# Where a small product stands in a long in-projection: decode rows in the middle of each unit, and 64 products ahead of the first tokens

## The chip, the cores and the metric

The kernel runs on one core of a Trainium2 chip. The time is device time in microseconds (us) of one launch, taken as the median of several runs; before the change it is 1346.13 us over 3 runs, which lie between 1345.68 and 1351.22. Engines are named as the profile names them: PE is the matmul engine (PEld its weight loads), DVE the vector engine, ACT the scalar engine, POOL the general engine and SP the one that issues most of the DMAs. A trailing q (SPq, ACTq) is an engine's instruction queue.

## What is computed

One step of a hybrid decoder layer, on a prompt of 2048 tokens and on eight decode rows (one new token each, with 512 cached positions in four pages). Both pass the same norm, the same input projection and the same output projection:

```python
def branch_inputs(x, g_norm, w_in, b_f, g_q, g_k, g_v):
    h = rms_norm(x, g_norm)
    p = h @ w_in
    q, k, v, fz, za, u, gv, zc = jnp.split(p, SPLIT_IDX, axis=-1)
...
def merge(x, attn, za, mix, u, zc, w_out):
    a = attn.astype(x.dtype).reshape(B, S, D_ATT) * jax.nn.silu(za)
    m = (u * mix.astype(x.dtype)).reshape(B, S, D_CHK) * jax.nn.silu(zc)
    return x + jnp.concatenate([a, m], axis=-1) @ w_out
```

`q`, `k` and `v` go into causal attention with a forgetting term (8 heads of 64), `gv` is normalised and mixed inside chunks of 128 positions by a lower triangular matrix for each of four groups. The model width is 1024, and `p` has 3592 columns. The outputs are the two results and the keys, values, log forget values and normalised `gv` rows.

## The kernel before

It has three phases: the in-projection (0 to about 590 us), the attention (to about 1160 us) and the output projection. The change is in the first.

**The in-projection.** The 3592 columns of `w_in` are cut into eight *units* (`SEGS`), which run in the order 3, 0, 1, 2, 4, 5, 6, 7; their widths are 392, 384, 384, 384 and then 512 each. Every float32 operand is split into a high and a low part, so that one product is three matmuls for each of the eight tiles `k` of 128 rows of the model width: high by high, low by high and high by low (`wh`, `wl` for weights, `hh`, `hl` for tokens). A product of 24 matmuls fills one PSUM bank with the tag `acc`; there are four such banks, and they are used in turn. So the product that comes fourth after another one takes the same bank, and it cannot start before the earlier one has been read out.

In units 3, 0, 1, 2 (`qkv_tile`) and 4 (`gv_tile`) a product is one tile of 128 tokens by the unit's columns. They go one tile after another, and only tiles 14 and 15 go side by side. In units 5, 6 and 7 the columns go to PSUM's partitions and 512 tokens lie along a bank: two `cp` halves by two `f` halves make four groups, each of two products side by side. In units 5 and 6 these are `u` (read out by DVE in L507) and `zc` (ACT, then DVE in L490), in unit 7 two of `za` (both ACT, then L490). `together` interleaves the products of a group step by step, one `k` of each in turn. In unit 4 and its follow-up the mixing products of `gv` (tag `pm`, eight matmuls of 256 columns) come between.

**The decode rows.** `sample_products` multiplies the eight decode rows, whose high and low parts lie side by side in `hTs`, by a unit's columns: 16 matmuls into one `acc` bank. ACT copies the half of the high rows (L377), DVE adds the other half (L378), and POOL stores the sum (L381). Before the change it is the first member of a unit's last group: with tiles 14 and 15, or with `cp` 1, `f` 1.

**Weights of the next unit.** `load_unit` is given in the middle of a unit. SP loads pieces of 128 rows into three buffers `raw` (L291); ACT or POOL makes the high part with the norm's gain (L253, L255), DVE the low part (L256). A unit's `wh` and `wl` take eight buffers of eleven, so some of the next unit's parts wait until PE has done the last group's product with the present ones.

**What sets the order.** PE's instructions stand in the order in which the program gives them. The program keeps a clock of the work given to PE (`Pe.clock`), and `later` puts other work at a due time on that clock. The order on the other engines comes from a scheduler that simulates a timeline while the program is built. Each engine then works its queue strictly in that order. From unit 4 on the scores of the decode rows against their cached keys run beside the in-projection: SP loads a page of keys `kb`, POOL multiplies (L660), DVE sums (L661).

Of the kernel before, what the change touches and what calls it, by code (L numbers as in the profile page):

```python
# [19 lines left out]
P = 128  # L20
# [3 lines left out]
NT = SEQ // P  # L24
# [11 lines left out]
NCP = 2  # L36
# [7 lines left out]
STLAG = 5000.0  # L44
STLAST = 2500.0
SLAG = 3000.0
LAG = 6400.0
AVB = 8
WK = 11
# [29 lines left out]
def hymba_step(ctx, tc, x_prompt, x_sample, cache_k, cache_v, cache_logf, page_table, g_norm, w_in,  # L79
# [32 lines left out]
    def tname(t):  # L112
        cnt[0] += 1
        return f"{t}_{cnt[0]}"

    def s8(dt=F32, t="s8"):
        return big.tile([P, 2048], dt, tag="s8", name=tname(t))

    def s4(dt=F32, t="s4"):
        return med.tile([P, D], dt, tag="s4", name=tname(t))  # L120
# [4 lines left out]
    def s2(dt=F32, t="s2"):  # L125
        return wk.tile([P, 512], dt, tag="t2", name=tname(t))
# [6 lines left out]
    def bank(tag, n=512):  # L133
        pool, bufs = pool_of[tag]
        return pool.tile([P, n], F32, tag=tag, bufs=bufs, name=tname(tag))
# [10 lines left out]
    def pe(ns):  # L146
        Pe.clock += ns

    def later(ns, fn):
        Pe.given += 1  # L150
        Pe.waiting.append((Pe.clock + ns, Pe.given, fn))
        Pe.waiting.sort(key=lambda w_: w_[:2])
# [20 lines left out]
    def mm(out, lhsT, rhs, start, stop, ns):  # L173
        Pe.last = nc.tensor.matmul(out, lhsT, rhs, start=start, stop=stop).ins  # L174
        pe(ns)

    def transpose(out, in_, idn):
        Pe.last = nc.tensor.transpose(out, in_, idn).ins  # L178
        pe(109)
# [9 lines left out]
    identb = const.tile([P, P], BF16, name="identb")  # L189
# [50 lines left out]
    def split(hi, lo, src, eng):  # L240

        if eng == "act":
            nc.scalar.copy(hi, src)  # L243
        elif eng == "dve":
            nc.vector.tensor_copy(hi, src)
        else:
            nc.gpsimd.tensor_scalar(hi, src, 1.0, 0.0, op0=ALU.mult, op1=ALU.add)
        nc.vector.tensor_tensor(lo, src, hi.bitcast(F32), op=ALU.subtract)  # L248
# [53 lines left out]
    def norm_tile(xa, xv, rows=P):  # L302
        nc.sync.dma_start(xv, xa)
        junk = wk.tile([P, D], BF16, tag="t2", name=tname("junk"))[:rows]
        ss = small(1)[:rows]
        nc.scalar.activation(junk, xv, AF.Square, bias=zero1[:rows], accum_out=ss)
        r = rstd_of(ss, 1, rows, 1.0 / D)
        nc.vector.tensor_scalar(xv, xv, r, None, op0=ALU.mult)
        return xv
# [3 lines left out]
    def norm_prompt(i):  # L313
        if i < NT - 4:
            if i % 2 == 0:
                xpair[i // 2] = s8(t="xp")
            xv = xpair[i // 2][:, (i % 2) * D:(i % 2 + 1) * D]
        else:
            xv = s4(t="xt")
        return norm_tile(x[i * P:(i + 1) * P], xv)  # L320
# [82 lines left out]
    def qkv_tile(u, unit, i):  # L403
# [7 lines left out]
        if m:  # L411
# [4 lines left out]
            def scale():  # L416
# [8 lines left out]
                def turn():  # L425
# [5 lines left out]
                    for src, dst in ((hi, qk_hi), (lo, qk_lo)):  # L431
                        nc.sync.dma_start(dst[f0:f0 + cols, t0:t0 + P].rearrange("(j p) t -> p j t", p=P),
                                          src.rearrange("p (j t) -> p j t", t=P).bitcast(F32))
                later(LAG + LAG2[i] - RLAG, turn)
            later(RLAG, scale)
# [11 lines left out]
    def gv_tile(unit, i):  # L447
# [24 lines left out]
        later(RLAG, scale)  # L472
        later(LAG + LAG2[i], mix)

# [451 lines left out]
    def shifts(h, c, part):  # L926
# [9 lines left out]
        def turn():  # L936
# [9 lines left out]
            later(3500, store)  # L946
        later(SLAG, turn)

# [218 lines left out]
    with ExitStack() as p1:  # L1167
        psa = p1.enter_context(tc.tile_pool(name="psa", bufs=2, space=PSUM, reuse_waits="tile"))
        pool_of.update(acc=(psa, 4), tp=(psa, 2), pm=(psa, 2))

        normd = {0: norm_prompt(0)}
        raws = [s8(t="wraw") for _ in range(2)]
        units = {order[0]: load_unit(SEGS[order[0]], [raws[k // 4][:, (k % 4) * 512:(k % 4 + 1) * 512]
                                                      for k in range(KT)],
                                     lambda: turn_tile(0, normd.pop(0)))}
        normd[1] = norm_prompt(1)
        nc.sync.dma_start(pt_sb, page_table.rearrange("b n -> (b n)").unsqueeze(0))
        nc.sync.dma_start(gqk[:, 0], g_q[0].partition_broadcast(P))
        nc.sync.dma_start(gqk[:, 1], g_k[0].partition_broadcast(P))
        nc.vector.tensor_scalar(gqk[:, 0], gqk[:, 0], -SCALE, None, op0=ALU.mult)  # L1180
        nc.sync.dma_start(bfb, b_f[0].partition_broadcast(P))
        nc.sync.dma_start(gvT, g_v[0].rearrange("(g c) -> c g", g=NG), allow_slow_non_contiguous=True)
        nc.sync.dma_start(bsb.rearrange("p g t -> p (g t)"),
                            b_s[0].rearrange("g t -> (g t)").partition_broadcast(P))
        nc.sync.dma_start(w00, w_s[0][:, 0, 0].partition_broadcast(DB), allow_slow_non_contiguous=True)

        wsr = s2(t="wsr")
        wsr3 = wsr.rearrange("t (g s) -> t g s", g=NG)
        nc.gpsimd.dma_start(wsr3, w_s[0].rearrange("g t s -> t g s"))
        nc.gpsimd.affine_select(wsr3, wsr3, pattern=[[0, NG], [-1, P]], compare_op=ALU.is_ge, fill=0.0,  # L1190
                                base=0, channel_multiplier=1)

        def mix_weights():
            wsp = bank("tp")
            for g in range(NG):
                transpose(wsp[:, g * P:(g + 1) * P], wsr[:, g * P:(g + 1) * P], ident)
            wsp3 = wsp.rearrange("s (g t) -> s g t", g=NG)
            split(wst[:, :, :P], wst[:, :, P:], wsp3, "act")

        for pos, u in enumerate(order):  # L1200
            unit = units.pop(u)
            nxt = order[pos + 1] if pos + 1 < len(order) else None
            group = []
            if u <= 4:
                for i in range(NT):
                    if pos == 0:
                        if i + 2 < NT:
                            normd[i + 2] = norm_prompt(i + 2)
                        if i + 1 == NT - 1:
                            pump(all_=True)  # L1210
                            turn_tile(i + 1, normd.pop(i + 1))
                        elif i + 1 < NT - 1:
                            later(TLAG if i else TLAG0, lambda i=i: turn_tile(i + 1, normd.pop(i + 1)))
                        if i == 2:
                            mix_weights()
                            sample = norm_tile(xs, s4(t="xt")[:DB], DB)
                            later(20000, lambda: turn_sample(sample))
                    group.append(qkv_tile(u, unit, i) if u <= 3 else gv_tile(unit, i))
                    if i == NT - 2:
                        group.insert(0, sample_products(unit, WID[u], SEGS[u]))  # L1220
                    if u == 4 and i == KSTART:
                        Pe.decode, Pe.steps = Pe.clock, chain(decode_qk(), decode_scores())
                    if i not in (PAIRS if pos else (NT - 2,)):
                        together(*group)
                        group = []
                    if i == (NT - 2 if pos == 0 else 7):
                        units[nxt] = load_unit(SEGS[nxt])
                if u == 3:
                    gates()
            else:  # L1230
                for cp in range(NCP):
                    for f in range(2):
                        if u < 7:
                            mx = s2(t="mxu")
                            of = 2 * (u - 5) + f
                            group = [u_steps(unit, f * P, of, cp, "acc", mx),
                                     zc_steps(unit, 256 + f * P, of, cp, "acc", mx)]
                        else:
                            group = [za_steps(unit, g * P, g, cp, "acc") for g in (2 * f, 2 * f + 1)]
                        if cp == NCP - 1 and f == 1:  # L1240
                            group.insert(0, sample_products(unit, WID[u], SEGS[u]))
                        together(*group)
                    if u == 7 and cp == 0:
                        heads[0] = load_keys(0)
                        load_values(heads[0])
                        fw = s8(F32R, "fw")
                        first.append(fill_weights(OZA, (fw[:, :D], fw[:, D:])))
                        Pe.side = Pe.clock + SSTART
                    if cp == 0 and nxt is not None:
                        units[nxt] = load_unit(SEGS[nxt])  # L1250
        for _ in Pe.steps:
            pass
        pump(all_=True)
# [79 lines left out]
```

## Time and profile before

| | |
|---|---|
| median of 3 runs | 1346.13 us |
| lowest and highest run | 1345.68, 1351.22 us |
| the profiled execution | 1347.51 us, its span 1345.8 us |
| mean granted clock of PE | 0.987 |
| PE, PEld, DVE, ACT, POOL busy | 97%, 75%, 53%, 32%, 43% of the span |
| chain of work that ended last | PE 85%, DMA 6%, DVE 4% |
| idle time of PE by releaser | 10.0 us for the first tokens, 4.9 us in three waits for L378, the rest in waits of at most 2.5 us |

The profile is of one execution. A row of its timeline gives the start, the duration, engine, line, operation, output and inputs, and in brackets the idle time of the engine just ahead with what ended it. Matmuls run into one another, so the cost of one in a row of them is the distance between two starts, and not its duration. A row of the waits gives who waited for whom, the sum in us, how many times, and the longest. A row of the windows gives, for a stretch of time, busy us (and instructions) of PE, PEld, DVE, ACT and POOL, then the clock that PE was granted, the share of the DMA engines and GB/s.

### The profile page before, as it was taken

To read this page: it belongs to the slowest core of one execution; us is meant where nothing else is said; L and a number is where in the kernel's file an instruction comes from. 1 tells how busy PE (TensorE), PEld (TensorE's weight loads), DVE (VectorE), ACT (ScalarE), POOL (GpSimd) and SP (SyncE) were. 2 spreads that over 40 slices of the span, in tenths; PEclk is the share of its full clock that TensorE was granted. 3 is DMA by queue.
4 is the path that set the end of the run, shared out by engine and by line. 5 is a ranking of instruction groups with operands and counts; after the bars stand their busy time and mean duration, and the time that the engine had idled before them with its cause. 6 is when DMAs were issued, how large, how long until landed. Compare 5 with 4: busy or idle time off the path is not lost.

```text
span 1345.8 us, 19516 instructions
## 1 busy us (share of the span) xinstructions
PE 1304.6 (97%) x6544; PEld 1006.6 (75%) x6544; DVE 706.9 (53%) x1328; ACT 433.1 (32%) x781; POOL 574.6 (43%) x679
## 2 busy tenths in 40 slices
PE   6999999999999999999999999999999998999998
PEld 5999999999887877866666566666656664688877
DVE  4346654534678544266586555566565774322321
ACT  5542332222222111114453344434444456310100
POOL 3113343423223554416776666676757466400000
PEclk9999999999999999999998899999999998999999
DMA  6644353555113665634254854666375645463221
GB/s 217 188 119 112 87 142 116 155 140 158 52 48 99 187 184 148 159 97 127 78 138 85 181 138 126 177 182 169 95 192 135 172 119 196 135 238 117 107 77 49
DMA packets 170805, 183.09 MB, mean 136 GB/s; under 512 B 39402, under 2 KB 125866, under 8 KB 169138
## 3 DMA queue, kind: packets, MB, share of 16 engines
q1 hardware_dynamic: 166818, 173.08, 46.7%
q10 hardware_dynamic: 3488, 8.39, 1.6%
q8 instruction: 52, 0.85, 0.3%
q14 instruction: 47, 0.39, 0.1%
q0 software_dynamic: 400, 0.38, 0.1%
HBM read 121.53 MB, written 60.28 MB: 135 GB/s over the span
## 4 chain that ended last, share of the span: by engine, by line
PE 85%; DMA 6%; DVE 4%; ACT 2%; issue 1%; SPq 1%; POOL 1%; ACTq 0%; DVEq 0%; POOLq 0%
PE acc L174 36%; PE sc L174 15%; PE av L174 14%; PE fl L174 10%; PE tp L174 5%; PE tp L178 3%; PE pm L174 1%; DVE mn L918 1%; ACT p L982 1%; DMA xp<-in_x_prompt_dram 1%; DMA raw<-in_w_in_dram 1%; DMA q<-qk_hi 1%; DMA k<-qk_lo 1%; DMA q<-qk_lo 1%; DMA mrow<-mt 0%
## 5 line engine op out<-in xcount | busy, mean ns | idle before, releaser
L982 ACT ACTIVATE p<-sc,zero 128x512 f32<-128x512 f32 (+1 forms) x320 | 196.6, 623 | 173.9 <-PE sc L174 167.9
L995 POOL TENSOR_TENSOR acc<-acc,p 128x512 f32<-128x512 f32 (+3 forms) x184 | 194.1, 1055 | 125.2 <-ACT p L982 104.1
L918 DVE TENSOR_REDUCE mn<-tp 128x1 f32<-128x384 f32 (+6 forms) x320 | 186.9, 604 | 107.9 <-PE tp L174 105.6
L174 PE MATMUL acc<-wh,hh 128*128 128x384 f32 (+2 forms) x640 | 228.7, 357 | 0.0
L174 PE MATMUL acc<-wl,hh 128*128 128x384 f32 (+2 forms) x640 | 222.8, 348 | 1.0 <-DVE wl L256 0.9
L174 PE MATMUL acc<-wh,hl 128*128 128x384 f32 (+2 forms) x640 | 222.6, 348 | 0.6 <-DVE hl L248 0.6
L174 PE MATMUL sc<-q,k 128*128 128x512 f32 (+7 forms) x640 | 211.1, 407 | 10.6 <-ACT p L982 5.9
L174 PEld LDWEIGHTS sc<-q,k 128*128 128x128 f32 (+1 forms) x640 | 118.2, 197 | 35.3 <-ACT p L982 16.3
L174 PE MATMUL av<-p,vst 128*64 128x512 f32 (+3 forms) x640 | 135.4, 543 | 0.0
L174 PEld LDWEIGHTS acc<-wh,hh 128*128 128x128 f32 x640 | 120.7, 189 | 7.2 <-ACT hh L243 0.2
L174 PEld LDWEIGHTS acc<-wl,hh 128*128 128x128 f32 x640 | 120.9, 189 | 6.3 <-DVE wl L256 2.0
L174 PEld LDWEIGHTS acc<-wh,hl 128*128 128x128 f32 x640 | 120.3, 188 | 6.3 <-DVE hl L248 1.2
L174 PE MATMUL tp<-k,q 66*128 66x384 f32 (+6 forms) x320 | 120.3, 392 | 3.9 <-DVE mn L918 3.3
L236 POOL TENSOR_SCALAR sm<-sm 128x6 f32<-128x6 f32 (+3 forms) x84 | 20.3, 241 | 238.8 <-DVE sm L389 170.4
L174 PEld LDWEIGHTS av<-p,vst 128*64 128x64 f32 x640 | 47.9, 137 | 67.1 <-issue 57.6
L237 POOL TENSOR_TENSOR sm<-sm,mhalf 128x6 f32<-128x6 f32 (+3 forms) x84 | 89.6, 1067 | 6.7
L174 PE MATMUL sc<-wo,am 128*128 128x512 f32 x360 | 84.5, 390 | 0.0
L174 PE MATMUL av<-wo,am 128*128 128x512 f32 x360 | 84.2, 389 | 0.0
L174 PEld LDWEIGHTS tp<-k,q 66*128 66x128 f32 x320 | 61.2, 193 | 26.6 <-DVE mn L918 6.6
L174 PE MATMUL acc<-hh,wh 128*128 128x512 f32 x192 | 76.3, 397 | 4.9 <-DVE s L378 4.9
L174 PEld LDWEIGHTS av<-wo,am 128*128 128x128 f32 x360 | 67.5, 188 | 14.2
L174 PEld LDWEIGHTS sc<-wo,am 128*128 128x128 f32 x360 | 67.4, 188 | 14.1
(218 smaller groups left out, 2087.2 us busy)
## 6 DMA issues: line engine op xcount, KB each, us to landing
raw<-in_w_in_dram SPq DMA_DIRECT2D x40, 256.0 KB
kb<-in_cache_k_dram SPq DMA_DIRECT2D x32, 256.0 KB
k<-qk_hi SPq DMA_DIRECT2D x16, 512.0 KB
q<-qk_hi SPq DMA_DIRECT2D x64, 128.0 KB
vb<-in_cache_v_dram SPq DMA_DIRECT2D x32, 256.0 KB
g<-gm SPq DMA_DIRECT2D x16, 512.0 KB
xy<-in_x_prompt_dram SPq DMA_DIRECT2D x16, 512.0 KB
out_dram<-xy ACTq DMA_DIRECT2D x15, 512.0 KB
```

The source lines that it names most:

```text
L174: Pe.last = nc.tensor.matmul(out, lhsT, rhs, start=start, stop=stop).ins
L178: Pe.last = nc.tensor.transpose(out, in_, idn).ins
L236: nc.gpsimd.tensor_scalar(r, ss, inv_n, EPS, op0=ALU.mult, op1=ALU.add)
L237: nc.gpsimd.tensor_tensor(r, r, mhalf[:rows, :n], op=ALU.pow)
L918: nc.vector.tensor_reduce(part[:, i % 4, n:n + 1], sp, axis=AX.X, op=ALU.min)
L982: nc.scalar.activation(p[:, n0:], sp[:, n0:], AF.Exp, bias=zero1, scale=-1.0)
L995: nc.gpsimd.tensor_tensor(acc[:, n0:], acc[:, n0:], p[:, n0:], op=ALU.add)
```

## The change

```diff
+WARM = 64
+SAT = 11
...
+        warm = bank("pm", P)
+        for _ in range(WARM):
+            mm(warm, identb, identb, True, True, 0)
         normd = {0: norm_prompt(0)}
...
                     group.append(qkv_tile(u, unit, i) if u <= 3 else gv_tile(unit, i))
-                    if i == NT - 2:
+                    if i == SAT:
                         group.insert(0, sample_products(unit, WID[u], SEGS[u]))
...
-                        if cp == NCP - 1 and f == 1:
+                        if cp == 0 and f == 1:
                             group.insert(0, sample_products(unit, WID[u], SEGS[u]))
                         together(*group)
```

In the five units of token tiles the decode rows' products go side by side with tile 11. In units 5, 6 and 7 they go with the second of the four groups. Nothing of them is removed. Besides, 64 products of a 128 by 128 bf16 identity with itself stand first on PE. They write a `pm` bank that nobody reads, and count as no time on the program's clock, so that `later` sees nothing of them. Because the decode rows come earlier on that clock, the due times of other work shift by up to 16 matmuls within a unit. In the changed program the lines up to 1172 have numbers higher by two (L378 is L380, L661 is L663, L507 is L509, L256 is L258, L174 is L176).

On DVE, around the decode rows' add of unit 4, the kernel before has:

```order
L661 TENSOR_REDUCE keep_4582<-kb_4585 128x8
L469 SCALAR_TENSOR_TENSOR mx_4607<-pm_4617,gvT,mx_4607 128x128
L256 SCALAR_TENSOR_TENSOR wl_4106<-raw_4107,gT,wh_4105 128x512
L256 SCALAR_TENSOR_TENSOR wl_4106<-raw_4112,gT,wh_4105 128x512
L661 TENSOR_REDUCE keep_4582<-kb_4633 128x8
L256 SCALAR_TENSOR_TENSOR wl_4118<-raw_4119,gT,wh_4117 128x512
L661 TENSOR_REDUCE keep_4582<-kb_4663 128x8
L256 SCALAR_TENSOR_TENSOR wl_4118<-raw_4124,gT,wh_4117 128x512
L378 TENSOR_TENSOR s_840_4707<-s_840_4707,acc_4532 8x512
L389 TENSOR_REDUCE sm_4713<-sq_4711 128x4
```

and the changed program:

```order
L471 SCALAR_TENSOR_TENSOR mx_4454<-pm_4455,gvT,mx_4454 128x128
L471 SCALAR_TENSOR_TENSOR mx_4454<-pm_4464,gvT,mx_4454 128x128
L469 SCALAR_TENSOR_TENSOR mx_4454<-pm_4464,gvT,bsb 128x128
L263 TENSOR_SCALAR sm_4477<-sm_4437 8x8
L471 SCALAR_TENSOR_TENSOR mx_4454<-pm_4464,gvT,mx_4454 128x128
L264 TENSOR_TENSOR sm_4477<-sm_4477,sm_4437 8x8
L380 TENSOR_TENSOR s_804_4499<-s_804_4499,acc_4390 8x512
```

The four splits of the next unit's weights (L256) and the key sums (L661) that stood ahead of the add are not ahead of it any more; in units 5 and 6 the splits go in the same way.

On DVE in the middle of unit 5, from the first group's reads to those of the second, the changed program has, with the reads of `u` (L509) and `zc` (L492) and the add (L380) among key sums (L663) and mixing (L469, L471), of which most are left out here:

```order
L663 TENSOR_REDUCE keep_4647<-kb_4829 128x8
L471 SCALAR_TENSOR_TENSOR mx_4861<-pm_4871,gvT,mx_4861 128x128
L469 SCALAR_TENSOR_TENSOR mx_4861<-pm_4871,gvT,bsb 128x128
L509 SCALAR_TENSOR_TENSOR mxu_4780<-mxu_4780,acc_4782 128x512
L471 SCALAR_TENSOR_TENSOR mx_4861<-pm_4871,gvT,mx_4861 128x128
L492 SCALAR_TENSOR_TENSOR sz_4906<-th_4905,acc_4800 128x512
...
L663 TENSOR_REDUCE keep_4647<-kb_4944 128x8
L663 TENSOR_REDUCE keep_4647<-kb_4974 128x8
L663 TENSOR_REDUCE keep_4647<-kb_5006 128x8
L663 TENSOR_REDUCE keep_4647<-kb_5036 128x8
L380 TENSOR_TENSOR s_877_5058<-s_877_5058,acc_4912 8x512
L509 SCALAR_TENSOR_TENSOR mxu_4911<-mxu_4911,acc_4916 128x512
```

The banks are taken in the order 4782 (`u`), 4800 (`zc`), 4912 (decode rows), 4916 (`u`), 4920 (`zc`), so 4920 is the bank of 4782, and the second product of the third group gets that of 4912. In the kernel before the same reads stand behind the same key sums:

```order
L661 TENSOR_REDUCE keep_4582<-kb_4761 128x8
L507 SCALAR_TENSOR_TENSOR mxu_4729<-mxu_4729,acc_4731 128x512
L469 SCALAR_TENSOR_TENSOR mx_4810<-pm_4820,gvT,mx_4810 128x128
L661 TENSOR_REDUCE keep_4582<-kb_4793 128x8
L490 SCALAR_TENSOR_TENSOR sz_4855<-th_4854,acc_4735 128x512
```

There the second group has two products, and no bank of the first group is asked for before the third group.

On PE the changed program ends its 64 products and goes on with the first tokens' transposes:

```order
L176 MATMUL pm_132<-identb 128x128
L176 LDWEIGHTS identb
L176 MATMUL pm_132<-identb 128x128
L180 MATMUL tp_223<-ident,xp_197 128x128 x4
L180 MATMUL tp_230<-ident,xp_197 128x128 x4
L176 MATMUL acc_286<-wh_208,hh_219 128x392
```

Before, the transposes were first. Each of the 64 loads its weights anew.

## The prediction

> **What bounds the kernel now.** I read the page first, then the table of waits of the matmul engine, and then the rows around the waits that this change can touch.
>
> ```profile
> span 1345.8 us, 19516 instructions
> PE 1304.6 (97%) x6544; PEld 1006.6 (75%) x6544; DVE 706.9 (53%) x1328; ACT 433.1 (32%) x781; POOL 574.6 (43%) x679
> PE 85%; DMA 6%; DVE 4%; ACT 2%; issue 1%; SPq 1%; POOL 1%; ACTq 0%; DVEq 0%; POOLq 0%
> ...
> PE tp L178 <- DVE xp L308: 10.0, 1, 10.0
> PE acc L174 <- DVE s L378: 4.9, 3, 2.7
> PE acc L174 <- DVE wl L256: 0.9, 2, 0.6
> ```
>
> PE is busy for 97% of the span and carries 85% of the chain. The change takes no product away and adds 64. It can gain only where PE stands still or runs slowly: the second wait is the one that the move is near, the first the one that the 64 products lie in. In all PE is idle for 1345.8 − 1304.6 = 41.2 us.
>
> The three waits for L378 are these (start, duration, and in brackets the idle time ahead with its releaser):
>
> ```profile
> 433.66 0.39 PE L174 MATMUL acc<-hh,wh 128*128 128x512 f32 x1
> ...
> 434.11 0.39 PE L174 MATMUL acc<-hh,wl 128*128 128x512 f32 x1
> 437.20 0.58 PE L174 MATMUL acc<-hh,wh 128*128 128x512 f32 x1 [2.70 <-DVE s L378]
> ...
> 440.95 0.39 PE L174 MATMUL acc<-hh,wh 128*128 128x512 f32 x1
> ...
> 488.30 0.39 PE L174 MATMUL acc<-hh,wl 128*128 128x512 f32 x1
> 490.10 0.50 PE L174 MATMUL acc<-hh,wh 128*128 128x512 f32 x1 [1.41 <-DVE s L378]
> 490.44 0.39 PE L174 MATMUL acc<-hl,wh 128*128 128x512 f32 x1
> ...
> 537.39 0.39 PE L174 MATMUL acc<-hh,wl 128*128 128x512 f32 x1
> 538.59 0.50 PE L174 MATMUL acc<-hh,wh 128*128 128x512 f32 x1 [0.81 <-DVE s L378]
> ```
>
> Each falls three products into a new unit (5, 6, 7). There the second product of the first group takes the PSUM bank that the decode rows' products held, since `acc` rotates over four banks, and that bank is free only after the copy L377 and the add L378. The matmuls run into one another, so what one costs is the distance of starts: (434.11 − 433.66) / 2 = 0.225 us at 512 columns. The losses are then 437.20 − 434.11 − 0.23 = 2.86, 490.10 − 488.30 − 0.23 = 1.57 and 538.59 − 537.39 − 0.23 = 0.97 us. The first has a tail:
>
> ```profile
> 437.00:441.00 4.00, 3.79 (x10) 2.97 (x11) 3.38 (x6) 0.77 (x2) 3.67 (x6) 0.57 0.83 243
> 441.00:445.00 4.00, 4.00 (x19) 3.33 (x18) 3.10 (x4) 1.19 (x2) 1.17 (x2) 1.00 0.32 91
> ```
>
> The figure after the engines is the granted clock: 0.57 for the four microseconds behind the wait, 1.00 after. From 437.20 to 440.95 nine matmuls took 3.75 us where nine at 0.23 take 2.05, so 1.70 more. Behind the 1.41 wait only one matmul is slow (490.10 to 490.44, 0.34 for 0.23), and I put the same 0.11 behind the third. The sum is 2.86 + 1.70 + 1.57 + 0.11 + 0.97 + 0.11 = 7.3 us.
>
> Why the bank came late is on the vector engine:
>
> ```profile
> 432.47 0.58 ACT L377 COPY s<-acc 8x512 f32<-8x512 f32 x1 [1.81 <-PE acc L174]
> ...
> 436.48 0.67 DVE L378 TENSOR_TENSOR s<-s,acc 8x512 f32<-8x512 f32 x1
> ...
> 439.56 0.75 DVE L256 SCALAR_TENSOR_TENSOR wl<-raw,gT,wh 128x512 fp32r<-128x512 f32 x1 [0.22 <-ACT wh L253]
> ...
> 443.28 0.74 DVE L256 SCALAR_TENSOR_TENSOR wl<-raw,gT,wh 128x512 fp32r<-128x512 f32 x1
> ...
> 491.94 0.75 DVE L256 SCALAR_TENSOR_TENSOR wl<-raw,gT,wh 128x512 fp32r<-128x512 f32 x1 [0.52 <-POOL wh L255]
> ```
>
> The copy was done at 433.05, the add began at 436.48: it stood in line behind the next unit's weight splits (L256) and the decode scores (L661), as the order of DVE shows.
>
> **The change, part by part.** The 128 decode-row products stay, so PE's work is the same up to each unit's border. In units 3, 0, 1, 2 and 4 they go with token tile 11; the bank is then asked for again four tiles later, and nothing waits. Moved out of the last group, L378 no longer has the splits ahead of it, and the three waits above lose their cause: **−7.3 us**. The two instructions and the store on POOL (L381) cost what they cost before, beside PE.
>
> *What the weights lose, first.* A last group of one unit frees the buffers of the next, k by k. With the decode rows one k took eight matmuls (1.82 us at 0.2275), without them six (1.37). Three k before the border is 5.46 us before and 4.10 after, so a split that starts when its buffer is freed comes 1.36 us later against the border. At the border to unit 5 the last split ended at 443.28 + 0.74 = 444.02. Without the stall PE needs it, 44 matmuls after 433.66, at 443.7. So 0.3 us come back if the vector engine sets the time, 0.3 + 1.36 = 1.7 if the freed buffer does; I take 0.7, nearer to the first, since DVE's queue is full there. At the border to unit 6 the last split ended at 491.94 + 0.75 = 492.7, and PE would want it 44 matmuls after 487.85, at 497.9: 5 us to spare, and nothing comes back; in unit 7 the splits were earlier still. At the four borders between narrower units I take 0.3 in all; the nearest row, the two waits for `wl` of at most 0.6, bounds them at 0 and 2.4.
>
> *What takes the place, second.* In the middle of units 5, 6 and 7 a group of three products now follows one of two. By the rotation its third product takes the bank of the first product of the group before, which L507 (L490 in unit 7) must have read, and the group after it asks for the decode rows' bank. Each has some 1.8 to 2 us (eight or nine matmuls) from the last matmul of the one to the first of the other. Before, these places had a whole group of slack. What DVE did there then:
>
> ```profile
> 450.44 0.69 DVE L661 TENSOR_REDUCE keep<-kb 128x8 f32<-128x512 f32 x1 [0.67 <-POOL kb L660]
> 451.05 0.68 DVE L507 SCALAR_TENSOR_TENSOR mxu<-mxu,acc 128x512 f32<-128x512 f32 x1
> ...
> 462.62 0.69 DVE L661 TENSOR_REDUCE keep<-kb 128x8 f32<-128x512 f32 x1 [2.04 <-POOL kb L660]
> 463.23 0.68 DVE L507 SCALAR_TENSOR_TENSOR mxu<-mxu,acc 128x512 f32<-128x512 f32 x1
> ...
> 500.20 0.69 DVE L661 TENSOR_REDUCE keep<-kb 128x8 f32<-128x512 f32 x1 [1.18 <-POOL kb L660]
> 500.81 0.68 DVE L507 SCALAR_TENSOR_TENSOR mxu<-mxu,acc 128x512 f32<-128x512 f32 x1
> ...
> 545.37 0.69 DVE L661 TENSOR_REDUCE keep<-kb 128x8 f32<-128x512 f32 x1 [5.64 <-POOL kb L660]
> 546.62 0.69 DVE L661 TENSOR_REDUCE keep<-kb 128x8 f32<-128x512 f32 x1 [0.56 <-POOL kb L660]
> ```
>
> The decode scores (L661) wait for cached keys, and the reads that PE now needs stand behind them. In unit 5 of the change the first group, 48 matmuls and the 8 mixing products (0.12 us apart, 0.96 in all, by the row below), ends about 433.66 + 48 × 0.2275 + 0.96 + the 0.7 for weights = 446.2, and five matmuls later, at 447.4, the third product asks for its bank.
>
> ```profile
> 447.07 0.28 PE L174 MATMUL pm<-wst,gvh 128*128 128x256 f32 x1
> 447.19 0.28 PE L174 MATMUL pm<-wst,gvl 128*128 128x256 f32 x1
> ```
>
> L507 ended at 451.05 + 0.68 = 451.73: 4.3 us of wait if the keys keep their pace. In the changed order of SP the key load ahead of it passes one weight earlier, worth up to 3.7 us (443.28 − 439.56); so 0.6 to 4.3 by these rows, or nothing if the keys catch up altogether, and I take 1.2. The decode rows' add stands behind the tenth L661; 462.62 + 0.69 + 0.67 = 464.0, where PE asks at 446.2 + 64 × 0.2275 + 0.96 + 3 × 0.23 = 462.4. That is 0 to 1.6, and less if PE has stood before; 0.4. In unit 6 L507 ended at 501.49 and PE would ask 53 matmuls after 487.85, at 501.6 with the old stall of 1.68, and earlier by that and by what unit 5 gained; 0 to 3, I take 0.3. In unit 7 the reads stand behind the thirtieth L661 instead of the thirty-first (546.62, for 547.86); 0 to 2, 0.3. Together **+0.7 + 0.3 + 1.2 + 0.4 + 0.3 + 0.3 = +3.2 us**, bounds 0 and 1.7 + 2.4 + 4.3 + 1.6 + 3 + 2 = 15.
>
> *The 64 products.* They need `identb`, and nothing runs on PE so early. The rows are that cast, the transposes of the first, second and third token tile, and (in the view of the tile `identb`) the load of the same operand as weights later, with its least, median and longest ns:
>
> ```profile
> 1.67 0.36 DVE L190 CAST identb<-ident 128x128 bf16<-128x128 f32 x1 [0.72 <-POOL ident masks.py:199]
> ...
> 9.99 1.97 PE L178 MATMUL tp<-ident,xp 128*128 128x128 f32 x8 [9.99 <-DVE xp L308]
> ...
> 14.63 1.04 PE L178 MATMUL tp<-ident,xp 128*128 128x128 f32 x8
> ...
> 19.49 1.15 ACT L306 ACTIVATE junk<-xp,zero 128x1024 bf16<-128x1024 f32 x1 [2.22 <-DMA xp<-in_x_prompt_dram]
> ...
> 22.58 1.07 PE L178 MATMUL tp<-ident,xp 128*128 128x128 f32 x8 [0.83 <-DVE fz_all L445]
> ...
> L174 PEld LDWEIGHTS <-identb x256: 95/96/149, 570.7 to 1165.6; 128*128 128x128 bf16 x128
> ```
>
> The first eight transposes take 1.97 / 8 = 0.246 us each, the next 0.13. By these two rows 64 products of 128 columns, begun when the cast ends at 2.03, end between 2.03 + 64 × 0.13 = 10.4 and 2.03 + 64 × 0.246 = 17.8; by the weight loads, of the very operand, at 2.03 + 64 × 0.096 = 8.2 to 2.03 + 64 × 0.149 = 11.6. That row is the nearest, so I cost them as hidden in the idle 9.99. What they may gain is 1.97 − 1.04 = 0.9 on the transposes and as much on the nine matmuls behind. But the third token tile's transposes at 22.58 hang on tokens that landed at 19.49, and PE already waited there. Gain at the end: 0 to 1.8, I take **−0.2**; loss, if they overrun, up to 17.8 − 9.99 − 0.8 = 7, kept for the range.
>
> [...]
>
> *The later phases.* They are the same work, but the order given by PE's clock shifts by a few positions. What one unlucky place costs:
>
> ```profile
> 723.57 0.50 PE L174 MATMUL tp<-k,q 66*128 66x512 f32 x1 [2.33 <-DVE mn L918]
> ...
> 725.00:730.00 5.00, 5.00 (x14) 3.57 (x14) 4.11 (x10) 1.97 (x4) 4.36 (x6) 0.50 0.29 91
> ```
>
> 2.3 us idle and then half the clock over at least 5 us, so 2.3 + 2.5 = 4.8. One such place may come or go: 0, with ±4.8.
>
> **The sum**: 1347.51 − 7.3 + 3.2 − 0.2 = 1343.2 for a profiled run. The median of the runs shown, 1346.13, stands 1.4 lower than the profiled one; by that the forecast is 1341.8, and I give **1342**.
>
> **The rivals.** First, nothing comes back and the start gains: −7.3 − 1.8 from 1346.13 is 1337. For it: the splits are out of the reads' way, and key loads may come sooner. Against it: the wait for keys of 5.64 and the slack of under 2 us.
>
> Second, the waits move rather than go: the terms above at nearly their upper ends, 1.7 + 4.3 + 1 = 7.0, and 1346, no change. For it: the 451.05 row. Against it: a weight less ahead of the key loads. That the 64 products do nothing because the clock falls again in the gap before 9.99 belongs to both cases, as it moves the sum by 0.2.
>
> Third, slower: the third product or the decode rows' read in the middle of units 5, 6 and 7 waits for keys in each, long enough for the clock to fall as at 437.20. Each then costs like that one, 2.86 + 1.70 = 4.6, and with 5.64 of wait (the unit-7 row) 5.6 + 1.7 = 7.3. Three at 4.6 plus 1.0 for weights make 14.8 against 7.5 gained: 1346.13 + 7.3 = 1353. It decides from about 4.6 us a place. For it: the key waits of 2 to 5.6 us lie in just these groups. Against it: a delay in unit 5 gives the keys the same time in unit 6, so that the three do not simply add up.
>
> **How the numbers follow.** A measurement of this kernel can tell some 0.5%, 6.7 us, from no change; the bounds are 1339.4 and 1352.9. The forecast case (1339 to 1345) has 0.48, all gain 0.25, waits that move 0.16, slower 0.11. Faster is the first rival's 0.25 and 0.05 from the lower end of the forecast case, 0.30. Slower is the third's 0.11 and 0.01 from the second with one more late place of 4.8, 0.12. The same is what is left, 0.58. The range reaches from below the first rival, 1335.5, to short of the third, 1351: about 0.1 stays out at either side. The likeliest case alone spans 1339 to 1345.
>
> **What would show it.** Right: no row of PE waiting for the decode rows' add at the three borders, a granted clock of 1.00 behind the border to unit 5, and short waits for `acc` in the middle of units 5 to 7 with DVE's key reduction ahead. If PE waits for `wl` at the border to unit 5, the weights' term is the one to read. The 22.58 transposes must stay at 22.58. Wrong: waits in the middle of a unit of over 2 us with a clock near 0.5 behind them (third rival), a first transpose later than 9.99 (overrun), or a second slow stretch in the attention.

## The result, and the profile after

The change made the kernel slower: 1366.25 us (median of 4 runs, 1361.96 to 1368.21) against 1345.91 (4 runs of before beside it), a ratio of 1.0138 with a 95% interval of 1.0105 to 1.0171. (The ratio is taken over all the runs; that of the two medians alone is 1.0151.) The prediction was 1342, with a range up to 1351. The profiled execution has a span of 1360.3 us, 14.5 more than before.

The page of the changed kernel:

```profile
span 1360.3 us, 19646 instructions
PE 1310.7 (96%) x6608; PEld 1007.4 (74%) x6608; DVE 711.3 (52%) x1328; ACT 430.9 (32%) x781; POOL 579.3 (43%) x679
PE 79%; DMA 6%; DVE 6%; issue 2%; POOL 2%; SPq 2%; ACT 1%; ACTq 0%; POOLq 0%; DVEq 0%
```

PE is 6.1 us busier, which is about what the 64 products take (6.29, below), and idle for 49.6 us instead of 41.2, although the idle time ahead of the first tokens is now filled. Dividing the span into stages shows where. The windows of the kernel before, ended at 24 us, after the last `acc` product, after the last attention value and at the end:

```profile
0.00:24.00 24.00, 12.18 (x60) 10.44 (x61) 11.61 (x23) 12.28 (x21) 9.75 (x25) 1.00 0.82 265
24.00:588.80 564.80, 558.26 (x3000) 500.61 (x2998) 296.39 (x633) 147.23 (x278) 189.53 (x247) 1.00 0.46 127
588.80:1168.90 580.10, 560.98 (x2719) 355.34 (x2718) 352.61 (x616) 258.85 (x467) 373.69 (x406) 0.97 0.54 143
1168.90:1345.80 176.90, 173.21 (x769) 140.17 (x768) 46.25 (x58) 14.71 (x17) 1.64 (x2) 1.00 0.36 125
```

and of the change, divided at the same work:

```profile
0.00:24.00 24.00, 17.15 (x124) 14.77 (x125) 11.27 (x23) 11.95 (x21) 9.80 (x25) 1.00 0.82 266
24.00:585.20 561.20, 555.98 (x2994) 499.13 (x2993) 294.97 (x627) 146.51 (x279) 190.21 (x248) 1.00 0.46 128
585.20:1178.60 593.40, 559.66 (x2704) 349.39 (x2702) 355.33 (x620) 257.69 (x466) 373.23 (x402) 0.97 0.51 137
1178.60:1360.30 181.70, 177.95 (x790) 144.13 (x789) 49.77 (x60) 14.71 (x17) 6.08 (x5) 1.00 0.39 131
```

The in-projection, where the change was made, ends 3.6 us earlier (585.2 for 588.8). The attention, which no line of the diff touches, is 13.3 us longer, and PE's idle time in it went from 580.1 − 561.0 = 19.1 to 593.4 − 559.7 = 33.7 us. The last stage is 4.8 longer because it has 21 matmuls more: output products that had filled waits in the attention now come behind it (21 × 0.227 = 4.8). Sum: −3.6 + 13.3 + 4.8 = 14.5. Over the attention the granted clock is 0.97 in both, so the loss there is mainly PE standing still and not a slower clock. (The 1.00 of the first row is no proof of a full clock at the start: the eight transposes at 9.99 took 1.97 us, those at 14.63 only 1.04.)

How the loss grows along the attention is in the view of the value tiles, with the first and the last start, before and after:

```profile
L174 PE MATMUL av<-p,vst x640: 272/592/1116, 607.1 to 1168.7; 128*64 128x512 f32 x128, 128*64 128x128 f32 x24, 128*64 128x256 f32 x8
L176 PE MATMUL av<-p,vst x640: 272/592/1116, 612.8 to 1178.4; 128*64 128x512 f32 x128, 128*64 128x128 f32 x24, 128*64 128x256 f32 x8
```

At the first value the change is 5.7 us behind, where the in-projection had left it 3.6 ahead; at the last value it is 9.7 behind. So 9.3 of the 18.1 us between −3.6 and +14.5 are lost before the first value, 4.0 over the rest of the attention, and the 4.8 behind it.

The in-projection first. PE's rows in the change:

```profile
2.08 6.29 PE L176 MATMUL pm<-identb 128*128 128x128 bf16 x64 [2.08 <-DVE identb L192]
10.02 1.09 PE L180 MATMUL tp<-ident,xp 128*128 128x128 f32 x8 [1.65 <-DVE xp L310]
...
22.62 1.06 PE L180 MATMUL tp<-ident,xp 128*128 128x128 f32 x8 [1.50 <-DVE fz_all L447]
...
436.38 0.39 PE L176 MATMUL acc<-hh,wh 128*128 128x512 f32 x1
...
451.43 0.51 PE L176 MATMUL acc<-hh,wh 128*128 128x512 f32 x1 [1.86 <-DVE mxu L509]
```

The 64 products end at 8.4. The first transposes take 1.09 us instead of 1.97, and the third tile's start at 22.62, for 22.58 before: what was gained ahead is waited for there. Nothing waits for the decode rows' add any more. The clock behind the border to unit 5 is full:

```profile
437.00:441.00 4.00, 4.00 (x19) 3.30 (x19) 3.40 (x4) 0.64 (x2) 2.08 (x3) 1.00 0.93 253
```

One wait came in its place, at 451.43, for the read of `u` behind a key sum. Unit 5 starts at 436.38 instead of 433.66. Two short waits for normalised rows in the narrower units (`nrm`, 1.1 us, in the table below) are a part of these 2.7 us.

Then the attention. Four lines of the table of PE's waits before:

```profile
PE sc L174 <- ACT p L982: 5.9, 10, 1.5
PE tp L174 <- DVE mn L918: 3.3, 4, 2.3
PE tp L178 <- DVE mx L934: 1.3, 1, 1.3
PE tp L178 <- POOL acc L995: 0.3, 1, 0.3
```

and in the change the same four, which all grew, with two that are new:

```profile
PE sc L176 <- ACT p L984: 10.7, 12, 3.5
PE tp L176 <- DVE mn L920: 4.7, 4, 3.5
PE tp L180 <- DVE mx L936: 3.5, 3, 2.0
PE sc L176 <- issue: 3.3, 1, 3.3
PE tp L180 <- POOL acc L997: 3.0, 2, 2.5
...
PE tp L180 <- DVE nrm L402: 1.1, 2, 0.6
```

The first new wait is at its very start. PE and SP there, in the change:

```profile
600.85 0.48 PE L176 MATMUL tp<-k,q 66*128 66x480 f32 x1 [0.34 <-ACT mt L942]
604.60 0.77 PE L176 MATMUL sc<-q,k 128*128 128x512 f32 x1 [3.27 <-issue]
...
606.20 0.80 PE L176 MATMUL sc<-q,k 68*128 68x512 f32 x1 [0.70 <-DMA q<-qk_lo]
...
595.05 0.45 SPq L884 DMA_DIRECT2D q<-qk_hi  x1
600.79 0.35 SPq L521 DMA_DIRECT2D zT<-sz  x1
601.20 0.45 SPq L885 DMA_DIRECT2D q<-qk_hi  x1
```

and the window behind it:

```profile
604.00:613.00 9.00, 7.70 (x26) 5.61 (x28) 1.31 (x2) 1.57 (x3) 1.27 (x1) 0.58 0.72 156
```

The queries are loaded in five pieces. Between the first and the second stands a store of the `za` gate (L521), which had to wait for DVE until 600.8, as the table of SP's waits from 594 to 602 says:

```profile
SPq L521 <- DVE sz L492: 5.2, 1, 5.2
```

So four pieces of the queries went out six microseconds late. PE stood for 4 us, and over the nine microseconds from there the granted clock was 0.58. In the kernel before, the five went out one behind the other:

```profile
594.45 0.45 SPq L882 DMA_DIRECT2D q<-qk_hi  x1
594.94 0.59 SPq L883 DMA_DIRECT2D q<-qk_hi  x1
```

### The profile page after: what moved, and what is told of

It is laid out like the page before. It is cut to its first block, busy times and chain, and to the rows that moved or that the text cites. A ratio compares the mean times of both kernels' runs of the same rounds, so it can differ in the third digit from the quotient of the medians.

```text
span 1360.3 us, 19646 instructions
## 1 busy us (share of the span) xinstructions
PE 1310.7 (96%) x6608; PEld 1007.4 (74%) x6608; DVE 711.3 (52%) x1328; ACT 430.9 (32%) x781; POOL 579.3 (43%) x679
## 4 chain that ended last, share of the span: by engine, by line
PE 79%; DMA 6%; DVE 6%; issue 2%; POOL 2%; SPq 2%; ACT 1%; ACTq 0%; POOLq 0%; DVEq 0%
PE acc L176 33%; PE sc L176 15%; PE av L176 14%; PE fl L176 9%; PE tp L176 5%; PE tp L180 3%; DVE mn L920 2%; PE pm L176 1%; DMA q<-qk_hi 1%; DMA q<-qk_lo 1%; DMA xp<-in_x_prompt_dram 1%; POOL sm L239 1%; ACT p L984 1%; DMA raw<-in_w_in_dram 1%; SPq L293 1%
## 5 line engine op out<-in xcount | busy, mean ns | idle before, releaser
L176 PE MATMUL acc<-wh,hh 128*128 128x384 f32 (+2 forms) x640 | 228.2, 357 | 0.7 <-ACT wh L255 0.4
L176 PE MATMUL sc<-q,k 128*128 128x512 f32 (+7 forms) x640 | 210.5, 407 | 15.5 <-ACT p L984 10.7
L176 PE MATMUL acc<-wh,hl 128*128 128x384 f32 (+2 forms) x640 | 222.3, 347 | 1.1 <-DVE hl L250 1.0
L176 PE MATMUL acc<-wl,hh 128*128 128x384 f32 (+2 forms) x640 | 222.4, 347 | 0.9 <-DVE wl L258 0.9
L176 PEld LDWEIGHTS sc<-q,k 128*128 128x128 f32 (+1 forms) x640 | 116.4, 197 | 41.5 <-ACT p L984 22.8
L176 PE MATMUL av<-p,vst 128*64 128x512 f32 (+3 forms) x640 | 139.4, 557 | 0.0
L176 PE MATMUL tp<-k,q 66*128 66x384 f32 (+6 forms) x320 | 120.3, 391 | 7.0 <-DVE mn L920 4.7
L176 PEld LDWEIGHTS acc<-wh,hh 128*128 128x128 f32 x640 | 120.3, 188 | 8.1 <-ACT wh L255 0.7
L176 PEld LDWEIGHTS acc<-wh,hl 128*128 128x128 f32 x640 | 120.1, 188 | 6.9 <-DVE hl L250 1.7
L176 PEld LDWEIGHTS acc<-wl,hh 128*128 128x128 f32 x640 | 120.5, 188 | 6.2 <-DVE wl L258 1.7
L176 PEld LDWEIGHTS av<-p,vst 128*64 128x64 f32 x640 | 49.1, 141 | 70.4 <-issue 61.5
L176 PE MATMUL sc<-wo,am 128*128 128x512 f32 x360 | 84.5, 390 | 0.0
L176 PEld LDWEIGHTS tp<-k,q 66*128 66x128 f32 x320 | 61.1, 191 | 31.1 <-DVE mn L920 9.6
L176 PE MATMUL av<-wo,am 128*128 128x512 f32 x360 | 84.0, 389 | 0.0
L176 PEld LDWEIGHTS av<-wo,am 128*128 128x128 f32 x360 | 67.6, 188 | 14.0
L176 PEld LDWEIGHTS sc<-wo,am 128*128 128x128 f32 x360 | 67.4, 188 | 14.2
L176 PE MATMUL acc<-hh,wh 128*128 128x512 f32 x192 | 75.6, 394 | 1.9 <-DVE mxu L509 1.9
```

## The experiments

Each kernel ran beside the kernel before on the same chip; medians of before differ a little between the three sets (1345.39, 1346.83, 1346.47), so the ratio to it is what compares.

### Unit 7 left as it was

An event in the program that ties the decode rows to the attention is in unit 7: when its first half has been given, the program sets `Pe.side = Pe.clock + SSTART`, the time on its clock from which attention maxima are mixed in. With the decode rows in that half, the event comes 16 × 512 × 0.422 = 3457 ns later on that clock.

```diff
-                        if cp == 0 and f == 1:
+                        if cp == (NCP - 1 if u == 7 else 0) and f == 1:
                             group.insert(0, sample_products(unit, WID[u], SEGS[u]))
```

> As the change, but unit 7's decode rows stay in its last group; the 64 products and the other seven units' moves are as in the change. The built order of every engine from the first attention score on is then the order of the kernel before. If the loss is the order of the attention (theory A): 1339 to 1344 us, about 5 below before, with the first attention score some 5 us earlier. If it is the moved products themselves or the 64 products (theory B): 1355 or more. If half of it is chance from run to run (theory C): 1350 to 1356.

Measured: 1344.78 us, ratio 0.9992 (0.9966 to 1.0017). The loss is gone, as by theory A, though the time lies just above its 1339 to 1344. But most of the gain is gone as well: the profiled span is 1342.1, 3.7 below before, and over the runs no difference can be told.

### The place and the order, taken apart

Two kernels part the place of unit 7's 16 products from their time on the program's clock.

```diff
+    def count_only(n):
+        for k in range(KT):
+            pe(2 * n * 0.422)
+            yield 1
+
-    def sample_products(unit, n, segs):
+    def sample_products(unit, n, segs, count=1):
...
-            mm(po[:40, :n], hTs[:, k], wh, k == 0, False, n * 0.422)
+            mm(po[:40, :n], hTs[:, k], wh, k == 0, False, count * n * 0.422)
...
-                            group.insert(0, sample_products(unit, WID[u], SEGS[u]))
+                            group.insert(0, sample_products(unit, WID[u], SEGS[u], count=int(u < 7)))
+                        if u == 7 and cp == NCP - 1 and f == 1:
+                            group.insert(0, count_only(WID[u]))
```

This is the first: all products in the place of the change, the clock in unit 7 as before. The second has the products of unit 7 in the last group, and `count_only` in the middle.

> As the change, with the decode rows moved in all eight units, unit 7 too, but in unit 7 the program's clock counts their time in the last group as before, so that the attention's order on every engine is that of the kernel before. Theory A (the order): 1339 to 1344 us. Theory B (the place in unit 7, its banks and its queues): 1360 to 1368, as the change.

> The reverse: unit 7's decode rows stand in its last group as before, but the clock counts their time in the middle as the change does, so that the attention's order is that of the change. Theory A (the order): 1360 to 1368 us. Theory B (the place): 1339 to 1344.

Measured: the place of the change with the order of before 1344.39 us (0.4 above theory A's range), ratio 0.9984 (0.9963 to 1.0004); the place of before with the order of the change 1362.40, ratio 1.0131 (1.0083 to 1.0180). PE's waits follow the order and not the place. With the order of the change:

```profile
602.59 0.80 PE L176 MATMUL sc<-q,k 128*128 128x512 f32 x1 [3.30 <-DMA q<-qk_hi]
...
732.89 0.45 PE L176 MATMUL tp<-k,q 66*128 66x416 f32 x1 [3.54 <-DVE mn L925]
...
934.55 1.07 PE L176 MATMUL sc<-q,k 128*128 128x512 f32 x2 [3.50 <-ACT p L989]
```

With the order of before and the place of the change, the first score is at 600.63 without a wait, and the next waits are those of before:

```profile
600.63 0.39 PE L176 MATMUL sc<-q,k 128*128 128x512 f32 x1
...
719.59 0.50 PE L176 MATMUL tp<-k,q 66*128 66x512 f32 x1 [2.31 <-DVE mn L925]
```

So the cause is shown. With unit 7's products in the last group, the order costs 1362.4 − 1344.8 = 17.6 us; with them in the middle, the ratios 1.0138 and 0.9984 differ by 1.5%, some 21 us. It is set off by a shift of 3.5 us on the clock that gives the order. With either order, the two places differ by less than the intervals (0.9992 and 0.9984; 1.0131 and 1.0138), so where the products stand in unit 7 costs nothing that these runs can tell.

The traces say how far the order goes. Of PE's 3433 products from the first score on, compared by their tiles' names, at least 492 must be moved to turn the order of before into that of the change; in the kernel with the clock of before none are.

### The same shift without any product

> The kernel before with one number changed: the first maxima begin 13457 ns of PE's clock after the middle of unit 7 instead of 10000, 3457 ns later, which is what the 16 decode-row products of unit 7 amount to on that clock. No product moves, and the 64 are left out. The attention's order is neither that of before nor that of the change. If this order is what is sensitive, whatever shifts it: 1353 us or more, with other waits than those of the change. If the loss belongs to the decode rows' place: 1344 to 1348.

Measured: 1361.73 us, ratio 1.0113 (1.0071 to 1.0155). One constant, with no product added or taken to another place in the program, costs 1.1%, which the intervals do not part from the 1.4% of the whole change.

> The kernel before with the first maxima begun 3457 ns of PE's clock earlier (6543 for 10000) and nothing else. The attention's order is a fourth one. If any other order is worse than that of before, since it was the one the numbers were set for: 1352 or more. If it depends on which way it shifts: 1342 to 1348.

Measured: 1348.61 us, ratio 1.0021 (1.0003 to 1.0038). My expectation of 1352 or more was wrong: the shift the other way costs two or three microseconds. So not every other order is bad by 15 to 18 us, and it is not the number of moved products that sets the price: by the same comparison the later start moves at least 397 of them, the earlier one 407. Whether a later start is always the worse one, these two shifts do not show. In the later one the first wait of the attention is the one of the change, longer:

```profile
607.41 0.76 PE L174 MATMUL sc<-q,k 128*128 128x512 f32 x1 [3.87 <-issue]
...
735.68 0.80 PE L174 MATMUL tp<-k,q 66*128 66x512 f32 x1 [3.90 <-DVE mn L918]
...
603.62 0.35 SPq L519 DMA_DIRECT2D zT<-sz  x1
```

The last row is why: here too a store of the `za` gate stands between the first piece of the queries (at 596.20) and the second (604.03).

### Taking single waits out of the changed order

```diff
-        nc.sync.dma_start(cols_of(zT, f, cp), twice_silu(po))
+        nc.gpsimd.dma_start(cols_of(zT, f, cp), twice_silu(po))
```

> The change with one more edit: the stores of the za gates (L521) are issued by POOL instead of SP. PE's order is that of the change to the last instruction; on SP the first attention queries no longer stand behind a store that waits for DVE. If that queue is what the wait of 3.3 + 0.7 us at 604 and the half clock behind it hang on (theory A, first piece): no such wait, first attention score near 601, and 1354 to 1360 us, 6 to 10 below the change. If PE waits there for something else: 1362 to 1368, as the change.

Measured: 1359.23 us, ratio 1.0080 (1.0057 to 1.0102). The queue was the cause of that wait: the first score is at 602.23 with no idle time ahead of it, and the first attention value at 606.6, 6.2 us earlier than in the change. But it was lost again: in the profiled execution the last value starts at 1178.5, for 1178.4 in the change, and both spans are 1360.3 us. That execution took 1362.27 us, where the ten of this kernel lie between 1353.35 and 1362.28; the change's took 1361.96, the lowest of its four. So the two profiles do not show the 0.6% between the ratios. The wait near 936 grew from 3.51 to 4.97 us; there ACT waits for the store of a small tile (`rt`) whose buffer it is to overwrite, PE for ACT. In this kernel:

```profile
935.53 0.80 PE L176 MATMUL sc<-q,k 128*128 128x512 f32 x1 [4.97 <-ACT p L984]
...
934.22 0.69 ACT L491 ACTIVATE th<-fl,zero 128x512 f32<-128x512 f32 x1 [5.92 <-DMA rT<-rt]
...
931.84 0.44 SPq L1030 DMA_DIRECT2D rT<-rt  x1
```

That wait I then took away too, by giving `rt` two buffers of its own:

```diff
-                            t = s2(t="rt")[:4, :P]
+                            t = wk.tile([P, P], F32, tag="rt", bufs=2, name=tname("rt"))[:4]
```

> As the kernel with the za gate stores on POOL, and besides the small row tile rt (L1027) has two buffers of its own instead of one of the eleven shared ones. PE's order is that of the change. In that kernel ACT waited 5.9 us at 934 for the store of rt before it could overwrite its buffer with th (L491), and PE 5.0 us behind it. If those shared buffers are the second piece of the loss: no wait over 1.5 us between 925 and 940, and 1350 to 1355 us. If something else is late there as well: 1357 to 1361.

Measured: 1357.43 us, ratio 1.0079 (1.0049 to 1.0108), the same as without it, and not the 1350 to 1355 expected. The 4.97 are gone, but another wait stands close by, at 930.65, where none over 1.5 us was expected, and one of 3.53 is new at 704:

```profile
704.00 0.37 PE L180 MATMUL tp<-ident,sm 128*4 128x128 f32 x1 [3.53 <-DVE mx L935]
...
930.65 0.37 PE L180 MATMUL tp<-ident,sm 128*4 128x128 f32 x1 [2.84 <-DVE sm L1021]
```

This kernel differs in more than that wait, though: PE's order is that of the change, but some instructions of DVE and ACT stand a few places elsewhere, and the new waits may come from that. So the loss of the change is not one wait. Of its 1.38% the stores on SP carry some four tenths (1.0138 to 1.0080 of the time before); the rest is spread over waits that move when one is taken out. Which of them hang together is not shown.

### The in-projection's parts

> The kernel before with the 64 products alone. If they are hidden in the wait for the first tokens: 1345 to 1346.3 us, 0 to 1 below before, with the third token tile's transposes still at 22.6 us. If they shorten the start: 1343.5 to 1344.5. If they are what costs the change its time: 1360 or more.

Measured: 1344.78 us, ratio 0.9991 (0.9973 to 1.0009). The 64 products alone are worth nothing that can be told. The third tile's transposes start at 22.99, not earlier than the 22.58 of before. In this execution their 5.82 us ended at 7.85, and the first transposes were as slow as without them:

```profile
10.03 1.97 PE L180 MATMUL tp<-ident,xp 128*128 128x128 f32 x8 [2.18 <-DVE xp L310]
```

> The decode rows moved in units 3, 0, 1 and 2 alone, with tile 11; all else as before, no 64 products, and the attention's order as before. If the move there costs short waits for the normalised rows (1 to 3 us, as the later start of unit 5 in the change suggests): 1347 to 1349. If it costs nothing: 1345 to 1346.5.

Measured: 1345.50 us, ratio 0.9989 (0.9973 to 1.0005). In its profile unit 5 starts 2.8 us later than before (436.5), as in the change, but the runs show no loss, which is the second of the two cases expected. (The profiled execution took 1348.85 us, the highest of its ten.)

### A version that beats both

```diff
-                    if i == NT - 2:
+                    if i == (SAT if u == 4 else NT - 2):
                         group.insert(0, sample_products(unit, WID[u], SEGS[u]))
...
-                        if cp == NCP - 1 and f == 1:
+                        if cp == (NCP - 1 if u == 7 else 0) and f == 1:
                             group.insert(0, sample_products(unit, WID[u], SEGS[u]))
```

> The decode rows moved in units 4, 5 and 6 alone, without the 64 products; units 3, 0, 1, 2 and 7 as before, and the attention's order as before. The three waits for the add at the borders should go (7.3 us), the 1.7 to 1.9 us wait in the middle of unit 5 stay, and the start of unit 5 be at 433.7 to 434.3, not at 436.4: 1339 to 1342 us. If the short waits of the narrower units are not from the move: 1341 to 1344.

Measured: 1340.56 us, ratio 0.9956 (0.9935 to 0.9976). It moves the decode rows only where a wait was: each of the three borders had it from the unit ahead, 4, 5 and 6. The border to unit 5 is reached at 433.38, for 433.66 before, and the wait in the middle of unit 5 is 1.07 us, shorter than the expected 1.7 to 1.9. In its windows the in-projection ends 5.7 us earlier, at 583.1, and the attention takes 578.7 us, for 580.1 before:

```profile
24.00:583.10 559.10, 555.53 (x2995) 498.91 (x2994) 296.91 (x633) 146.72 (x277) 189.84 (x247) 1.00 0.46 129
583.10:1161.80 578.70, 557.46 (x2719) 352.12 (x2718) 355.94 (x616) 258.47 (x467) 374.17 (x406) 0.98 0.55 143
```

Why the kernels that move more, with the order of before, gained less (0.9992 and 0.9984) is not shown. In their profiles unit 5 starts at 436.45 and 437.31, some three to four microseconds later than here, but the moves in units 3, 0, 1 and 2 alone cost nothing that the runs can tell.

> The decode rows moved in units 4, 5 and 6 alone, now with the 64 products. The start waits for the third token tile either way, so the 64 should change nothing: 1339.5 to 1341.5, beside 1340.6 without them. If they are worth something: 1338 to 1339.5.

Measured with the 64 products: 1342.69 us, ratio 0.9965 (0.9945 to 0.9985), above the expected 1341.5, but within the intervals the same as without them.

## Why the prediction was wrong

The forecast was 1342 and a gain of 4 to 5 us; the kernel lost 20. Step by step:

- **The three waits** (−7.3): right. No row waits for the decode rows' add at the borders, and the clock behind the border to unit 5 is 1.00. The kernel that moves only units 4, 5 and 6 shows it with least beside it: 5.7 us at the end of the in-projection, with 1.7 us of new waits for L509 in it, and 6.3 over the runs (1346.83 − 1340.56).
- **What the weights lose** (+0.7, +0.3): no row of the change waits for `wl` at the border to unit 5, so 0 for the first. The second was too small in the trace: unit 5 starts 2.7 us later. Waits for normalised rows cover 1.1 us of it; where the rest comes from is open, and the runs with this move alone show no loss.
- **What takes the place** (+1.2, +0.4, and 0.3 each in units 6 and 7): right in place and about in size. The third product of the second group in unit 5 waited for L509 behind a key sum, 1.86 us for the 1.2 taken; the others were 0.
- **The 64 products** (−0.2): nothing here speaks against it. They ended at 8.4, inside the bounds by the weight loads (8.2 to 11.6), nothing was late, and the 22.6 stayed; the runs with them alone can tell neither a gain nor a loss (0.9991).
- The first phase in all: forecast −4.3, measured −3.6 in the profile.
- **The later phases** (0, ±4.8): this is the step that failed. The prediction said that they are the same work with an order shifted "by a few positions", and priced that as one lucky or unlucky place. It measured +13.3 in the attention and +4.8 behind it, 18.1 for at most 4.8, and at least 492 of 3433 products stand elsewhere. The text ahead of the prediction has the due times shift "within a unit"; in unit 7 that is not so. There the clock is read when the attention's start is set (`Pe.side`), and 3.5 us on it change the order from the first score to the end. I had seen that the order changes, but not asked which event of the program changed it, and whether all of the attention hangs on that event. That the order is the cause is shown by the pairs of kernels above; that `Pe.side` alone carries it is argued from the program and from the kernel where its constant alone is shifted.
- The rivals: the slower one (chance 0.11) put the loss in the middle of units 5 to 7, at waits for keys. It was not there; that it had the direction right was luck. The closing part did name "a second slow stretch in the attention" as what would make the forecast wrong, but without a mechanism or a chance that fitted it.

## What to carry to other kernels

Where a program gives work by its own clock and a scheduler orders the rest by a simulated one, a move of work is two changes: the place, and every due time behind it. Part them before pricing, by moving the work and leaving its time on the clock where it was; here the place was worth a gain of 1 us, which the runs cannot tell from nothing, and 6 us where only the useful moves were made, and the time on the clock was worth a loss of 18 to 21 us. And move only what a wait was seen behind: the two kernels with just those three of the eight moves are the only ones that the runs show to be faster.

## What the runs showed of the hardware

The speed behind an idle stretch was not given by its length alone. In the kernel with the 64 products alone, behind them and an idle 2.18 us, the first eight transposes took 1.97 us; in the kernel that moves units 4, 5 and 6, with the same 64 products, the idle time was longer (2.57 us), and the eight took 1.09:

```profile
10.09 1.09 PE L180 MATMUL tp<-ident,xp 128*128 128x128 f32 x8 [2.57 <-DVE xp L310]
```

In the kernel before, the clock fell to half behind an idle 2.70 us: taken by half microseconds, the granted clock is 0.98 from 437.00, 0.50 in each of the six from 437.50 to 440.50, 0.61 in the next and 1.00 from 441.00. So 3.0 of the four microseconds whose mean is 0.57 were at half clock throughout.
